# Widening the second score product of differential attention from 64 to 128 contraction rows, in a hybrid decoder layer

## The chip, the cores and the metric

The kernel runs on one core of one Trainium2 chip. The metric is device time in microseconds (us), from the start of the program to its end. The layer has a batch of one, 1024 tokens and a model width of 1024; inputs and outputs are float32.

## The reference: what is computed

One layer normalises the tokens, projects them once with `w_in`, and sends the columns of the projection to three groups of four heads each: mLSTM (a chunkwise matrix memory), differential attention, and cross-attention over 256 memory tokens. Each group is gated by a SiLU of its own columns. The three results are concatenated, mapped back by `w_out`, added to the input and normalised again. The part that the change touches is differential attention:

```python
# q, k: (B, H, 2, S, 64); v: (B, H, S, 128)
for j in range(S_ // Q_BLOCK):                     # 8 blocks of 128 queries
    lo, hi = j * Q_BLOCK, (j + 1) * Q_BLOCK
    s = einsum('bhmqd,bhmkd->bhmqk', q[:, :, :, lo:hi], k[:, :, :, :hi]) * scale
    p = softmax(where(mask, s, -inf), axis=-1)
    pd = p[:, :, 0] - lam * p[:, :, 1]
    outs.append(einsum('bhqk,bhkd->bhqd', pd, v[:, :, :hi]))
```

A head has two maps (m = 0 and 1) with 64 query and key dimensions each. Their softmaxes are subtracted with a learned weight, and the difference is applied to values of width 128. Block j looks at the keys up to its own end, (j+1)·128 of them.

## The kernel before

**Precision by parts.** Most float32 products are made from two rounded parts of each operand. A part "hi" is the value rounded to the multiplier's float32r format, a part "lo" is what the rounding left out. A projection (`proj_T`, L144, and `proj_N`, L153) is 8 contraction blocks times three products (hi·hi, hi·lo, lo·hi): 24 matrix products into one accumulator.

**Order of the work.** The program is written as a list of helper calls, and the framework's planner orders the instructions of every engine by a timeline simulation of its own. On each engine the resulting order is fixed: TensorE (PE) carries out its list strictly in order. So the written order is a priority, and the projections of a later step are used to fill TensorE between the attention blocks of an earlier one. All loads and stores go out from one in-order queue, SyncE's (SP). A tile comes from a pool with a number of buffers per tag (`BUFS`, L27); an instruction that first writes a tile waits until the buffer's last user is done, a DMA included.

**Stages.** First come norms, transposes and the memory cross-attention (L310 to L374), then the value projections `vd_cols` (L473), then differential attention head by head (L493 to L502), then the mLSTM projections (`xm_proj`, `kv_block`, `qk_head`, `gates`, `om_cols`, `zm_half`, L504 to L668), and last, for each of 8 token blocks, the mLSTM chunk, the output projection and the final norm (L679 to the end).

**Differential attention.** `diff_proj(h)` (L380) makes the operands of a head. The query tile `QA[h][m]` has 128 partitions: 64 hold the hi part of map m's queries and the other 64 their lo part. The key tile `KA[h][m]` holds the hi part of the keys in both halves. So one product over 128 partitions gives q_hi·k_hi + q_lo·k_hi (L416). The lo part of the keys, `KB[h]`, is one tile for both maps, map 0 in partitions 0 to 63 and map 1 in 64 to 127; a second product over those 64 partitions adds q_hi·k_lo (L417). A third, in bfloat16, adds the causal mask to the last 128 columns (L419). The key accumulator `kd` is read out by four copies on ScalarE (L397) and, before the change, two subtractions on VectorE (L398) for each half of the tokens.

`diff_block(h, j)` (L400) then takes, for each map, the row maximum (VectorE, L420), its negative scaled (L421), the exponential with row sums (ScalarE, L423), scales and subtracts the two maps (L425 to L429; GpSimd takes L427), transposes the result on TensorE (L436), copies it to SBUF (L438, L440) and multiplies it with the values (L443). The blocks of a head go in the order 0, 7, 1, 6, 2, 5, 3, 4. A score tile of 1024 columns is computed in pieces of up to 512 columns. The score tile has two PSUM buffers, the projections' accumulator `pj` two, all other products two.

**Buffers that the change moves.** Tag `qk` (1032 columns a buffer, 11 of them) holds `QA`, `KA` and `KB`, and before and after that stage the cross-attention's operands, the mLSTM's `xm`, `xcv`, `xh`, `xl`, and in the last stage the chunk's loads (`kvc`, `t1`, `rbc`), `soz` and `xr`. Tag `g` (512 columns, 7 buffers) holds the gates: `szd` (L452, from the gate's projection until `diff_finish` has stored the gated head, L469), `so` (L489), `szm` (L664), and `skc` (L745, loaded for each token block and freed by L763).

Of the kernel before, what the change touches and what calls it, by code (L numbers as in the profile page):

```python
# [8 lines left out]
F32 = mybir.dt.float32  # L9
F32R = mybir.dt.float32r  # L10
BF16 = mybir.dt.bfloat16
AF = mybir.ActivationFunctionType
ALU = mybir.AluOpType
# [10 lines left out]
CS = float(P) ** -0.5  # L24
POOL_LO = ("wkm0", "wkm1")

BUFS = {"h": 16, "w": 8, "g": 7, "qk": 11, "vd": 4, "p": 4, "pT": 2, "od": 2}  # L27
WIDE = ("qk", "od")
C_XM, C_OM, C_ZM, C_QD, C_KD, C_VD, C_ZD, C_QC, C_ZC = [512 * i for i in range(9)]

# [2 lines left out]
def hybrid_layer(ctx: ExitStack, tc: tile.TileContext, x, mem, norm_g, w_in, conv_w, conv_b, wq_m, wk_m,  # L33
# [3 lines left out]
    act, dve, pool, pe = nc.scalar, nc.vector, nc.gpsimd, nc.tensor  # L37
    load = nc.sync.dma_start
    store = nc.sync.dma_start
    x, mem, w_in, w_mem_kv, w_out, out = x[0], mem[0], w_in[0], w_mem_kv[0], w_out[0], out[0]  # L40
# [8 lines left out]
    def slot(tag, name, dt=F32, n=1024):  # L49
        tile_ = big.tile([P, max(n, 1032) if tag in WIDE else n], dt, tag=tag, bufs=BUFS[tag], name=name)  # L50
        return tile_[:, :n] if tag in WIDE else tile_
# [7 lines left out]
    def po(name):  # L59
        return ps.tile([P, 512], F32, tag="o", name=name)  # L60

    def pbig(name):
        return ps.tile([P, 1024], F32, tag="s", name=name)
# [66 lines left out]
    def load_w(tag):  # L130
        i = [e[0] for e in stream].index(tag)
        fetch_w(i + 1 + (tag != "wzc1"))
        kk, wtag = stream[i][2:4]
        hi, lo = [slot(wtag, f"{tag}{part}", F32R) for part in range(2)]
        split_w(hi, lo, raws[tag], pool if tag in POOL_LO else None)
        return [v.rearrange("p (k c) -> p k c", k=kk) for v in (hi, lo)]
# [7 lines left out]
    def proj_T(w, t, tag):  # L144
        acc = pj(tag)
        n = 0
        for k in range(8):
            for wp, hp in ((0, 0), (0, 1), (1, 0)):
                pe.matmul(acc, lhsT=w[wp][:, k, :], rhs=hT_ap(t, k, hp, 0, 512), start=n == 0, stop=n == 23)  # L149
                n += 1  # L150
        return acc
# [14 lines left out]
        store(out=Y[4 * t:4 * t + 4, :, kt, :].rearrange("b p s -> p b s"),  # L166
              in_=ap.rearrange("p (b s) -> p b s", b=4))

# [1 line left out]

    def norm_transpose(src, blocks, g_, tag, sink):
        gbc, gsrc = g_
# [200 lines left out]
        for t in range(2):  # L373
            cross_core(h, t)  # L374

# [1 line left out]
    lo64, hi64 = slice(0, 64), slice(64, 128)  # L377
    QA, KA, KB, od_, ssq_, zg = {}, {}, {}, {}, {}, {}

    def diff_proj(h):  # L380
        w = load_w(f"wqd{h}")
        q = QA[h] = [slot("qk", f"QA{h}{m}", F32R) for m in range(2)]
        for t in range(2):
            c = slice(t * 512, t * 512 + 512)
            acc = proj_T(w, t, f"qd{h}{t}")
            for m, src, oth in ((0, lo64, hi64), (1, hi64, lo64)):
                act.activation(q[m][src, c], acc[src], AF.Copy)
                dve.tensor_tensor(out=q[m][oth, c], in0=acc[src], in1=q[m][src, c].bitcast(F32), op=ALU.subtract)
        w = load_w(f"wkd{h}")
        ka = KA[h] = [slot("qk", f"KA{h}{m}", F32R) for m in range(2)]  # L390
        kb = KB[h] = slot("qk", f"KB{h}", F32R)
        for t in range(2):
            c = slice(t * 512, t * 512 + 512)
            acc = proj_T(w, t, f"kd{h}{t}")
            for m, src, oth in ((0, lo64, hi64), (1, hi64, lo64)):
                for dst in (src, oth):
                    act.activation(ka[m][dst, c], acc[src], AF.Copy)  # L397
                dve.tensor_tensor(out=kb[src, c], in0=acc[src], in1=ka[m][src, c].bitcast(F32), op=ALU.subtract)  # L398

    def diff_block(h, j):  # L400
        if h not in od_:
            od_[h] = slot("od", f"od{h}", n=1032)[:, :1024].rearrange("p (b c) -> p b c", b=NB)
            ssq_[h] = sm.tile([P, NB], F32, tag="dssq", name=f"dssq{h}")
        od, ssq = od_[h], ssq_[h]
        n = (j + 1) * P
        nb = sm.tile([P, 2], F32, tag="dnb", name=f"dnb{h}{j}")
        sums = sm.tile([P, 2], F32, tag="dsum", name=f"dsum{h}{j}")
        pp = []
        for m in range(2):
            sc = pbig(f"ds{h}{j}{m}")  # L410
            lhs = QA[h][m][:, j * P:(j + 1) * P]
            hi = (lo64, hi64)[m]
            for c0 in range(0, n, 512):
                w_ = min(512, n - c0)
                last = c0 + w_ == n
                pe.matmul(sc[:, c0:c0 + w_], lhsT=lhs, rhs=KA[h][m][:, c0:c0 + w_], start=True, stop=False)  # L416
                pe.matmul(sc[:, c0:c0 + w_], lhsT=lhs[hi], rhs=KB[h][hi, c0:c0 + w_], start=False, stop=not last)  # L417
                if last:
                    pe.matmul(sc[:, n - P:n], lhsT=identb, rhs=maskb, start=False, stop=True)  # L419
            dve.tensor_reduce(out=nb[:, m:m + 1], in_=sc[:, :n], op=ALU.max, axis=AX.X)  # L420
            dve.tensor_scalar(out=nb[:, m:m + 1], in0=nb[:, m:m + 1], scalar1=-0.125, scalar2=None, op0=ALU.mult)  # L421
            p_ = slot("p", f"dp{h}{j}{m}")
            act.activation(p_[:, :n], sc[:, :n], AF.Exp, scale=0.125, bias=nb[:, m:m + 1], accum_out=sums[:, m:m + 1])  # L423
            pp.append(p_)
        dve.reciprocal(out=sums, in_=sums)  # L425
        dve.tensor_tensor(out=sums[:, 1:2], in0=sums[:, 1:2], in1=nlam, op=ALU.mult)  # L426
        pool.tensor_scalar(out=pp[1][:, :n], in0=pp[1][:, :n], scalar1=sums[:, 1:2], scalar2=0.0, op0=ALU.mult,  # L427
                           op1=ALU.add)
        dve.scalar_tensor_tensor(out=pp[0][:, :n], in0=pp[0][:, :n], scalar=sums[:, 0:1], in1=pp[1][:, :n],  # L429
                                 op0=ALU.mult, op1=ALU.add)  # L430
        pT = slot("pT", f"dpT{h}{j}")
        for g in range(0, j + 1, 4):
            cnt = min(4, j + 1 - g)
            pt = po(f"dpt{h}{j}{g}")
            for i in range(cnt):
                pe.transpose(out=pt[:, i * P:(i + 1) * P], in_=pp[0][:, (g + i) * P:(g + i + 1) * P], identity=ident)  # L436
            if g:
                dve.tensor_copy(out=pT[:, g * P:(g + cnt) * P], in_=pt[:, :cnt * P])  # L438
            else:
                act.activation(pT[:, g * P:(g + cnt) * P], pt[:, :cnt * P], AF.Copy)  # L440
        acc = po(f"dov{h}{j}")[:, :P]
        for i in range(j + 1):
            pe.matmul(acc, lhsT=pT[:, i * P:(i + 1) * P], rhs=vd[h][:, i, :], start=i == 0, stop=i == j)  # L443
        dve.tensor_copy(out=od[:, j, :], in_=acc)
        sq = sm.tile([P, P], F32, tag="dsq", name=f"dsq{h}{j}", bufs=2)
        act.activation(sq, acc, AF.Square, accum_out=ssq[:, j:j + 1])
# [24 lines left out]
    vd = [slot("vd", f"vd{h}").rearrange("p (b c) -> p b c", b=NB) for h in range(H)]  # L471
# [8 lines left out]
    vd_cols(0, wvd0)  # L480
    vd_cols(1)
    diff_proj(0)
    SOd = [dr.tile([P, 512], F32, name=f"SOd{b}") for b in range(NB)]

    def om_cols(cg):
        w2 = load_w256(f"wom{cg}")
        for b in range(NB):
            acc = proj_N(w2, b, f"om{cg}{b}")
            so = half(f"so{cg}{b}")[:, :256]  # L489
            sigmoid(so, acc, so)  # L490
            store(out=SOd[b][:, cg * 256:(cg + 1) * 256], in_=so)

    for h in range(H):  # L493
        for i, j in enumerate((0, 7, 1, 6, 2, 5, 3, 4)):
            diff_block(h, j)
            if h and i == 2:
                diff_finish(h - 1)
        if h + 1 < H:
            diff_proj(h + 1)
        diff_z(h)  # L500
        if h == 2:
            om_cols(0)  # L502
# [1 line left out]
    xm, xcv = [], []  # L504
    for h in range(H):
        xm.append(slot("qk" if h < 3 else "vd", f"xm{h}"))
# [160 lines left out]
            store(out=SZd[t][:, :, h * P:(h + 1) * P].rearrange("b p s -> p b s"),  # L667
                  in_=sg.rearrange("p (b s) -> p b s", b=4))  # L668

# [1 line left out]
    fg = slot("p", "fg")  # L671
    load(out=fg, in_=final_g.partition_broadcast(P))
    hs = lambda a, h, o=0, n=P, st=P: a[:, o + h * st:o + h * st + n]
# [219 lines left out]
```

## Time and profile before

| | |
|---|---|
| median of 3 runs | 839.0 us (838.33 to 842.41) |
| span of the profiled execution, first to last instruction | 835.7 us |
| median less that span | 3.3 us |
| TensorE matrix products / weight loads, busy | 800.3 us / 662.9 us |
| VectorE / ScalarE / GpSimd, busy | 440.2 us / 323.8 us / 192.8 us |
| mean granted TensorE clock | 0.993 |

The profiled execution's time is known by its span alone; 3.3 us is what the median run has more. Busy shares of TensorE have to be read with care: a matrix product's record runs from its start to a modelled end, so records of neighbours overlap, and what a product really takes of TensorE is the distance from its start to the start of the next. In the listings below "PE" is a matrix product, "PEld" a weight load, DVE VectorE, ACT ScalarE, POOL GpSimd, SPq the queue of DMA issues; an idle time behind a row in brackets names what ended it, and "issue" means that the profile shows nothing that the engine waited for.

### The profile page before, as it was taken

To read this page: it belongs to the slowest core of one execution; us is meant where nothing else is said; L and a number is where in the kernel's file an instruction comes from. 1 tells how busy PE (TensorE), PEld (TensorE's weight loads), DVE (VectorE), ACT (ScalarE), POOL (GpSimd) and SP (SyncE) were. 2 spreads that over 40 slices of the span, in tenths; PEclk is the share of its full clock that TensorE was granted. 3 is DMA by queue.
4 is the path that set the end of the run, shared out by engine and by line. 5 is a ranking of instruction groups with operands and counts; after the bars stand their busy time and mean duration, and the time that the engine had idled before them with its cause. 6 is when DMAs were issued, how large, how long until landed. Compare 5 with 4: busy or idle time off the path is not lost.

```text
span 835.7 us, 11762 instructions
## 1 busy us (share of the span) xinstructions
PE 800.3 (96%) x4432; PEld 662.9 (79%) x4432; DVE 440.2 (53%) x906; ACT 323.8 (39%) x753; POOL 192.8 (23%) x248
## 2 busy tenths in 40 slices
PE   4899999999999999999999999999999789999996
PEld 3788888899977777777789777899878668878886
DVE  5785235343235555655653566654562588666532
ACT  3335234331134444434545434554565333122211
POOL 5433123121111111311312411241323252221000
PEclk9999999999999999999999999999999999999999
DMA  9920212112110000011021111024788999664001
GB/s 254 305 81 18 84 51 76 48 50 68 51 51 26 26 25 27 26 51 38 25 83 56 40 43 59 26 88 159 230 267 292 285 304 302 215 174 156 25 26 51
DMA packets 106416, 89.09 MB, mean 107 GB/s; under 512 B 10480, under 2 KB 91376, under 8 KB 106360
## 3 DMA queue, kind: packets, MB, share of 16 engines
q1 hardware_dynamic: 106216, 88.08, 34.3%
q8 instruction: 35, 0.57, 0.3%
q10 hardware_dynamic: 144, 0.26, 0.1%
q14 instruction: 21, 0.17, 0.1%
HBM read 65.23 MB, written 23.10 MB: 106 GB/s over the span
## 4 chain that ended last, share of the span: by engine, by line
PE 86%; DMA 7%; DVE 2%; SPq 2%; issue 1%; ACT 1%; POOL 1%; POOLq 0%; DVEq 0%; ACTq 0%
PE op L805 13%; PE om L158 5%; PE qd L149 5%; PE kd L149 5%; PE zd L149 5%; PE xm L149 5%; PE vd L158 5%; PE qc L149 5%; PE zc L149 5%; PE zm L149 4%; PE ds L417 4%; PE dov L443 4%; DMA rbc<-RBd 4%; PE ds L416 3%; PE dpt L436 2%
## 5 line engine op out<-in xcount | busy, mean ns | idle before, releaser
L805 PE MATMUL op<-wo,yh 128*128 128x512 f32 (+1 forms) x272 | 83.6, 390 | 1.1 <-DVE szm L666 1.1
L423 ACT ACTIVATE dp<-ds,dnb 128x128 f32<-128x128 f32 (+7 forms) x64 | 47.2, 740 | 68.6 <-DVE dnb L421 62.4
L420 DVE TENSOR_REDUCE dnb<-ds 128x1 f32<-128x128 f32 (+7 forms) x64 | 48.1, 755 | 46.3 <-PE ds L419 46.0
L427 POOL TENSOR_SCALAR dp<-dp,dsum 128x128 f32<-128x128 f32 (+7 forms) x32 | 24.9, 777 | 171.4 <-DVE dsum L426 136.1
L805 PEld LDWEIGHTS op<-wo,yh 128*128 128x128 f32 x272 | 50.5, 192 | 11.7 <-DVE szm L666 1.5
L158 PE MATMUL om<-wom,hT 128*128 128x256 f32 x384 | 54.4, 290 | 0.0
L805 PE MATMUL op<-wo,yl 128*128 128x512 f32 (+1 forms) x136 | 53.0, 390 | 0.0
L149 PE MATMUL qd<-hT,wqd 128*128 128x512 f32 x192 | 50.0, 404 | 0.0
L149 PE MATMUL zd<-hT,wzd 128*128 128x512 f32 x192 | 49.7, 404 | 0.0
L149 PE MATMUL xm<-hT,wxm 128*128 128x512 f32 x192 | 49.6, 404 | 0.0
L149 PE MATMUL zm<-hT,wzm 128*128 128x512 f32 x192 | 47.6, 397 | 2.0 <-POOL wzm L87 2.0
L149 PE MATMUL kd<-hT,wkd 128*128 128x512 f32 x192 | 49.4, 402 | 0.0
L805 PE MATMUL op<-wo,ymr 128*128 128x512 f32 (+1 forms) x204 | 48.3, 384 | 0.0
L158 PEld LDWEIGHTS om<-wom,hT 128*128 128x128 f32 x384 | 48.1, 189 | 0.0
L149 PE MATMUL qc<-hT,wqc 128*128 128x512 f32 x192 | 48.0, 397 | 0.0
L149 PE MATMUL zc<-hT,wzc 128*128 128x512 f32 x192 | 47.5, 397 | 0.0
L158 PE MATMUL vd<-wvd,hT 128*128 128x256 f32 x384 | 47.4, 282 | 0.0
L158 PEld LDWEIGHTS vd<-wvd,hT 128*128 128x128 f32 x384 | 46.3, 188 | 0.3
L149 PEld LDWEIGHTS zm<-hT,wzm 128*128 128x128 f32 x192 | 36.0, 189 | 10.9 <-POOL wzm L87 2.5
L805 PEld LDWEIGHTS op<-wo,ymr 128*128 128x128 f32 x204 | 36.8, 188 | 8.0
L417 PE MATMUL ds<-KB,QA 64*128 64x512 f32 (+3 forms) x96 | 42.2, 439 | 0.0
L149 PEld LDWEIGHTS zc<-hT,wzc 128*128 128x128 f32 x192 | 35.5, 188 | 8.0
(331 smaller groups left out, 1659.9 us busy)
## 6 DMA issues: line engine op xcount, KB each, us to landing
wor<-in_w_out_dram SPq DMA_DIRECT2D x12, 512.0 KB, 5.6
xx<-in_x_dram SPq DMA_DIRECT2D x8, 512.0 KB, 5.9
KVd<-kv SPq DMA_DIRECT2D x8, 512.0 KB, 2.7
QKd<-qkt SPq DMA_DIRECT2D x16, 256.0 KB, 5.1
kvc<-KVd SPq DMA_DIRECT2D x16, 256.0 KB, 7.1
yr<-Yd SPq DMA_DIRECT2D x8, 512.0 KB, 7.7
t<-QKd SPq DMA_DIRECT2D x8, 512.0 KB, 6.3
rbc<-RBd SPq DMA_DIRECT2D x16, 256.0 KB, 9.4
```

Of the source, the lines that this page charges most:

```text
L149: pe.matmul(acc, lhsT=w[wp][:, k, :], rhs=hT_ap(t, k, hp, 0, 512), start=n == 0, stop=n == 23)
L158: pe.matmul(acc, lhsT=hT_ap(b // 4, k, hp, (b % 4) * P, P), rhs=w2[k // 4][wp][:, k % 4, :], start=n == 0, stop=n == 23)
L416: pe.matmul(sc[:, c0:c0 + w_], lhsT=lhs, rhs=KA[h][m][:, c0:c0 + w_], start=True, stop=False)
L417: pe.matmul(sc[:, c0:c0 + w_], lhsT=lhs[hi], rhs=KB[h][hi, c0:c0 + w_], start=False, stop=not last)
L420: dve.tensor_reduce(out=nb[:, m:m + 1], in_=sc[:, :n], op=ALU.max, axis=AX.X)
L423: act.activation(p_[:, :n], sc[:, :n], AF.Exp, scale=0.125, bias=nb[:, m:m + 1], accum_out=sums[:, m:m + 1])
L427: pool.tensor_scalar(out=pp[1][:, :n], in0=pp[1][:, :n], scalar1=sums[:, 1:2], scalar2=0.0, op0=ALU.mult, op1=ALU.add)
L436: pe.transpose(out=pt[:, i * P:(i + 1) * P], in_=pp[0][:, (g + i) * P:(g + i + 1) * P], identity=ident)
L443: pe.matmul(acc, lhsT=pT[:, i * P:(i + 1) * P], rhs=vd[h][:, i, :], start=i == 0, stop=i == j)
L805: pe.matmul(accs[nh][:, c0:c0 + n_], lhsT=yp[a_], rhs=wo[kp, nh, b_][:, o:o + n_], start=k == 2 * KORD[0] and n == 0, stop=k == 2 * KORD[- ...
```

## The change

`KB` becomes one tile for each map, and each holds the lo part of the keys in both halves of its partitions. The second score product then contracts over all 128 partitions with the whole query tile, and gives q_hi·k_lo + q_lo·k_lo. The subtraction that makes `KB` is issued four times for each accumulator, not two. A head holds six `qk` buffers for its operands, not five. To make room, tag `g` has 5 buffers in place of 7, and `qk` 12 in place of 11.

```diff
-BUFS = {"h": 16, "w": 8, "g": 7, "qk": 11, "vd": 4, "p": 4, "pT": 2, "od": 2}
+BUFS = {"h": 16, "w": 8, "g": 5, "qk": 12, "vd": 4, "p": 4, "pT": 2, "od": 2}
...
-        kb = KB[h] = slot("qk", f"KB{h}", F32R)
+        kb = KB[h] = [slot("qk", f"KB{h}{m}", F32R) for m in range(2)]
         for t in range(2):
...
             for m, src, oth in ((0, lo64, hi64), (1, hi64, lo64)):
                 for dst in (src, oth):
                     act.activation(ka[m][dst, c], acc[src], AF.Copy)
-                dve.tensor_tensor(out=kb[src, c], in0=acc[src], in1=ka[m][src, c].bitcast(F32), op=ALU.subtract)
+                for dst in (src, oth):
+                    dve.tensor_tensor(out=kb[m][dst, c], in0=acc[src], in1=ka[m][src, c].bitcast(F32),
+                                      op=ALU.subtract)
...
             lhs = QA[h][m][:, j * P:(j + 1) * P]
-            hi = (lo64, hi64)[m]
...
-                pe.matmul(sc[:, c0:c0 + w_], lhsT=lhs[hi], rhs=KB[h][hi, c0:c0 + w_], start=False, stop=not last)
+                pe.matmul(sc[:, c0:c0 + w_], lhsT=lhs, rhs=KB[h][m][:, c0:c0 + w_], start=False, stop=not last)
```

## The prediction

> **What bounds the kernel now.** I read the engines' shares first, then the chain of work that ended last, then the busy times by stretch, cut at the first and the last score product.
>
> ```profile
> span 835.7 us, 11762 instructions
> ...
> PE 800.3 (96%) x4432; PEld 662.9 (79%) x4432; DVE 440.2 (53%) x906; ACT 323.8 (39%) x753; POOL 192.8 (23%) x248
> ...
> PE 86%; DMA 7%; DVE 2%; SPq 2%; issue 1%; ACT 1%; POOL 1%; POOLq 0%; DVEq 0%; ACTq 0%
> ```
>
> ```profile
> 243.90:521.10 277.20, 277.20 (x1447) 211.52 (x1445) 154.07 (x324) 124.65 (x306) 58.05 (x75) 1.00 0.14 41
> 0.00:243.90 243.90, 227.78 (x1380) 200.90 (x1381) 109.76 (x178) 81.28 (x205) 61.40 (x78) 1.00 0.32 95
> 521.10:600.00 78.90, 78.90 (x525) 71.78 (x525) 40.60 (x70) 42.34 (x85) 23.16 (x24) 1.00 0.33 114
> 600.00:760.00 160.00, 147.03 (x729) 120.19 (x727) 105.05 (x255) 62.03 (x123) 44.09 (x62) 0.97 0.83 254
> ```
>
> The columns of the second view are the stretch, its length, busy times of PE, PEld, DVE, ACT and POOL, the granted clock, the DMA engines' share and GB/s. In the 277.2 us from 243.9 to 521.1, where all score products lie, PE is never without a product in flight, at full clock, while DVE is busy 154.07 us of it (56%), ACT 124.65 and the DMA engines 14%. TensorE alone sets the time there, so what a product costs it is paid in full. The stretch from 600 to 760 is another matter: DMA engines 83% busy, PE idle for 160 − 147.0 = 13 us.
>
> A full PE need not be an efficient one. The waits of the weight loads in the attention stretch show it; "issue" means that nothing in the profile accounts for the wait:
>
> ```profile
> PEld ds L417 <- issue: 20.0, 74, 0.4
> ...
> PEld ds L416 <- issue: 7.1, 29, 0.2
> ...
> PEld L419 <- issue: 6.7, 31, 0.3
> ```
>
> The weight loader stands still for 20.0 us ahead of the 64-row load of L417 (74 times), and for 7.1 and 6.7 us ahead of the loads of L416 and L419, 33.8 us in all. The timelines of the loads and of the products around 270 us show where:
>
> ```profile
> 270.58 0.18 PEld L417 LDWEIGHTS ds<-KB,QA 64*128 64x128 f32 x1 [0.36 <-issue]
> 271.00 0.19 PEld L416 LDWEIGHTS ds<-KA,QA 128*128 128x128 f32 x1 [0.24 <-issue]
> ```
>
> ```profile
> 270.26 0.39 PE L416 MATMUL ds<-KA,QA 128*128 128x512 f32 x1
> 270.58 0.50 PE L417 MATMUL ds<-KB,QA 64*128 64x512 f32 x1
> 271.01 0.45 PE L416 MATMUL ds<-KA,QA 128*128 128x384 f32 x1
> 271.38 0.44 PE L417 MATMUL ds<-KB,QA 64*128 64x384 f32 x1
> 271.75 0.23 PE L419 MATMUL ds<-maskb,identb 128*128 128x128 bf16 x1
> 271.79 0.48 PE L416 MATMUL ds<-KA,QA 128*128 128x512 f32 x1
> ```
>
> The load of the 64-row weights begins only at 270.58, 0.32 us after the 128-row product began, and the next 128-row load only at 271.00, 0.42 us after the 64-row one began. Going from 128 rows to 64, and back, is not overlapped. Products of 128 rows follow each other faster; three rows of the chain give their pace:
>
> ```profile
> 64.84 5.60 PE qc L149 x24
> ...
> 193.68 28.16 PE vd L158 x240
> ...
> 397.42 0.89 PE dov L443 x8
> ```
>
> That is 233 ns for 512 columns, 117 ns for 256 and 111 ns for 128. For 384 no row stands; 175 ns is the middle of 117 and 233.
>
> **The change part by part.** *The second product.* After the change L417 has the form that L416 has. Whether it then streams at the pace above, although it has L416's own weights and adds into the same accumulator, can be read where the mLSTM's product does the same: `xh` and `xl` take the same weights, one after the other.
>
> ```profile
> 597.54 0.39 PE L550 MATMUL qk<-xh,wqk 128*128 128x512 f32 x1
> 597.77 0.40 PE L550 MATMUL qk<-xl,wqk 128*128 128x512 f32 x1
> 598.01 0.39 PE L550 MATMUL qk<-xh,wqk 128*128 128x512 f32 x1
> ```
>
> 0.23 and 0.24 us from start to start: full pace. So I cost each piece, now and after, by starts. A piece of 512 with more behind it (270.26 to 271.01) takes 0.75 us and will take 2 × 0.233 = 0.466: −0.28. A second piece of 384 (271.01 to 271.75) takes 0.74, will take 0.35: −0.39. Narrow blocks, from the first score product to the mask product:
>
> ```profile
> 262.49 0.28 PE L416 MATMUL ds<-KA,QA 128*128 128x256 f32 x1
> ...
> 263.01 0.23 PE L419 MATMUL ds<-maskb,identb 128*128 128x128 bf16 x1
> ...
> 280.87 0.34 PE L416 MATMUL ds<-KA,QA 128*128 128x384 f32 x1
> ...
> 281.50 0.23 PE L419 MATMUL ds<-maskb,identb 128*128 128x128 bf16 x1
> ...
> 313.21 0.30 PE L416 MATMUL ds<-KA,QA 128*128 128x128 f32 x1
> ...
> 313.70 0.23 PE L419 MATMUL ds<-maskb,identb 128*128 128x128 bf16 x1
> ```
>
> 256 columns take 0.52 us, will take 0.234: −0.29. 384 take 0.63, will take 0.35: −0.28. 128 take 0.49, will take 0.22: −0.27. For one map of one head the eight blocks then save 0.27 (j=0) + 0.29 + 0.28 + 0.28 (j=3, one piece of 512) + 0.55 (j=4, 512 and 128) + 3 × 0.67 (j=5 to 7, where I take the 0.28 + 0.39 of j=6 for all three) = 3.68 us. Times 2 maps and 4 heads: **29.4 us**. The loader's 33.8 us of standing still is a bound from above; the 20.0 us ahead of L417 alone, if the other two stalls should stay, is the bound from below.
>
> *The mask product* (L419) stays. Its price behind a 128-row product shows once, where the planner put it behind L443:
>
> ```profile
> 282.72 0.71 PE L443 MATMUL dov<-vd,dpT 128*128 128x128 f32 x4
> 283.27 0.22 PE L419 MATMUL ds<-maskb,identb 128*128 128x128 bf16 x1
> 283.30 0.48 PE L149 MATMUL zd<-hT,wzd 128*128 128x512 f32 x1
> ```
>
> The next product starts 0.03 us after it, against 0.04 us at 271.75, so I count no difference.
>
> A page of the Trainium skill speaks against this step: "TensorE: Matmul & The Clock Gate", Part 3 (packing small matmuls), says that a weight load overlaps a product in flight only where the two use different row groups. By it a load for all 128 rows could never hide behind a 128-row product, and the change would save nothing here. The trace does not agree: the products of L149 start 0.233 us apart (5.60 us for 24), less than one load and one stream end to end would need.
>
> *The added subtractions.* 16 more of this row:
>
> ```profile
> L398 DVE TENSOR_TENSOR KB<-kd,KA 64x512 fp32r<-64x512 f32 x16 | 11.0, 687 | 8.3 <-ACT KA L397 8.1
> ```
>
> 16 × 0.687 = 11.0 us on DVE. DVE goes from 154.07 to 165 us in a stretch of 277 − 29 = 248 us, 67%: the load is covered by PE's other work. What can show is latency. ACT and DVE take turns on the accumulator, so `kd` is given back 2 × 0.687 = 1.4 us later, and the head's first scores may be 1.4 us later, each for 8 accumulators. The tightest place that I found is head 3, whose last subtraction and whose buffer's next user (the second `zd` product) are:
>
> ```profile
> 402.71 0.69 DVE L398 TENSOR_TENSOR KB<-kd,KA 64x512 fp32r<-64x512 f32 x1
> ...
> 405.94 0.94 PE L149 MATMUL zd<-hT,wzd 128*128 128x512 f32 x3
> ```
>
> 405.94 − 403.40 = 2.5 us of slack, less 1.4, less some 0.6 that two narrower scores between them save: 0.5 us is left. If the cover were gone everywhere it would cost 8 × 1.4 = 11 us; with slack left even there the sum is nearer to nothing, and I take 1.5 us.
>
> *The buffers.* During attention two heads need 12 `qk` buffers, as they needed 10 of 11: still two heads, no spare. In `g`, two heads' `szd` hold four, which leaves one for `so` while the output gates of `om_cols(0)` fill PE, not three: a microsecond or two on ACT, covered by 2.8 us or more of PE for each accumulator (24 × 0.117). In the last stage a 12th `qk` buffer lets a chunk's load go out sooner, and two `g` buffers fewer make `szm` and `skc` wait for each other. Neither has a row that prices it; the bound to both sides is one late load of the chain:
>
> ```profile
> 644.36 11.39 DMA rbc<-RBd
> 658.15 10.48 DMA rbc<-RBd
> ```
>
> From −10.5 to +11.4 us, taken as 0, since the two pull in opposite ways. All of the planner's order is made anew, too, which no row can price; I hold it to be inside these bounds.
>
> The sum is 835.7 − 29.4 + 1.5 = 807.8 us of span, and with the 3.3 us by which the median run (839.0) exceeds the profiled span **811 us**.
>
> **The rivals.** *Given back to VectorE.* DVE carries out its list in order, and a `KB` subtraction that the planner places ahead of a due row maximum (L420) delays that block's exponential by 0.69 us. If all 16 land so and PE, now faster, waits each time, the whole 11.0 us shows: 839.0 − 29.4 + 1.5 + 11.0 = 822 us. For it speaks the two-buffer score tile; against it DVE at 67%, and that PE now waits for nothing in the stretch.
>
> *The relief does not come.* If the load of L417 waits because it comes second on weights in use, and not because of its 64 rows, nothing is saved: 839.0 + 1.5 = 840 us. For it speaks only that every L417 follows L416 or fillers of the same array; the L550 rows speak against it. (This is what the rule of the Trainium skill named above would make of it.)
>
> *A better last stage.* If the 12th buffer takes the shorter of the two `rbc` waits off the chain: 811 − 10.5 = 801 us.
>
> *Slower: the gate buffers block SP's queue.* Before, seven `g` buffers take `szm` and the loads of `skc` up to block 7 without waiting:
>
> ```profile
> L746 SPq DMA_DIRECT2D skc<-SKd x8: 319/424/2034, 620.9 to 678.9; - x8
> ```
>
> All eight are issued by 678.9 us. With five, `skc5` to `skc7` wait until an earlier block has used its own, and if the planner puts them ahead of a chunk's loads in the in-order queue, `kvc`, `t` and `rbc` behind them are late by as much. From the point at which three chunks each lose one 11.39 us load, it costs 34 us: 811 + 34 = 845 us. Against it: the planner knows the buffers and can issue later, when DMA is less loaded.
>
> **How the numbers follow.** The forecast, 811 us (own range 802 to 820: the 20.0 and 33.8 us bounds of the saving give 820.5 and 806.7, and half of the last stage's bound goes below), has a chance of 0.63; VectorE's 822 0.17; the better last stage 0.07; no relief 0.06; slower 0.07. The range 798 to 828 takes in the first three with some room and leaves out 0.13 and the far ends of the others. What a measurement of this kernel can tell from no change is about 0.5%, 4.2 us: faster by more 0.87, within it 0.06 (no relief), slower 0.07.
>
> **What would show it.** Right, if in the profile after the L417 products read 128*128 and start 0.23 us after L416 at 512 columns, if the weight loader's idle "issue" time at L416, L417 and L419 is nearly gone, if first to last score product takes some 248 us with PE still without waits, and if the stage behind keeps its length. Wrong, if L417 keeps 0.4 us from start to start (no relief); if PE shows waits for DVE `dnb`, `KB` or ACT `dp` (VectorE); if after the mLSTM projections PE's idle time grows by tens of us with SP waiting at L746 (gate buffers).

## The result

The changed kernel takes 819.4 us (819.14 to 819.9) against 840.7 us for the kernel before: a ratio of 0.9755, interval 0.9731 to 0.9779. Forecast were 811 us, in a range of 798 to 828. The direction, the cause and the range held; the gain is 21 us (0.0245 × 840.7 = 20.6), not 28, so some 7 us of the forecast gain are to be found.

### The profile after

The page of the changed kernel, span, engines and chain:

```profile
span 817.7 us, 11784 instructions
...
PE 770.1 (94%) x4432; PEld 663.9 (81%) x4432; DVE 445.2 (54%) x922; ACT 322.3 (39%) x753; POOL 192.6 (24%) x248
...
PE 76%; DMA 11%; DVE 4%; issue 3%; POOL 2%; SPq 2%; ACT 2%; POOLq 0%; DVEq 0%; ACTq 0%
```

TensorE's share of the chain has fallen from 86% to 76% and the transfers' has risen from 7% to 11%. The lines of the score products are now L417 (first), L418 (second) and L420 (mask). The timeline of PE at the block with two pieces of 512 columns, and at the narrowest block:

```profile
239.81 0.22 PE L417 MATMUL ds<-KA,QA 128*128 128x128 f32 x1
239.87 0.28 PE L418 MATMUL ds<-KB,QA 128*128 128x128 f32 x1
239.98 0.23 PE L420 MATMUL ds<-maskb,identb 128*128 128x128 bf16 x1
...
245.69 0.39 PE L417 MATMUL ds<-KA,QA 128*128 128x512 f32 x1
245.92 0.39 PE L418 MATMUL ds<-KB,QA 128*128 128x512 f32 x1
246.15 0.62 PE L417 MATMUL ds<-KA,QA 128*128 128x512 f32 x2
```

The second product now follows the first after 0.23 us, as every 128-row product does, where the 64-row one came 0.32 us after it and held the next back by 0.43 us. The narrow block takes 0.17 us up to its mask, in place of 0.49. The weight loader's waits in the attention stretch of the changed kernel say the same:

```profile
PEld L420 <- issue: 6.1, 28, 0.3
PEld ds L417 <- ACT dp L424: 1.7, 1, 1.7
```

The 20.0 us ahead of the second product and the 7.1 us ahead of the first are gone. The 6.7 us ahead of the mask's load stay, as 6.1 us: this stall does not belong to the 64 rows.

To see where the time went I divided both profiles at the same four events: the first and last score product, and the first and last product of the `zm` gates. The last two stretches, before and after (columns: stretch, length, busy PE, PEld, DVE, ACT, POOL, clock, DMA share, GB/s):

```profile
583.60:648.30 64.70, 62.64 (x286) 50.17 (x284) 31.73 (x40) 38.43 (x64) 19.71 (x18) 0.97 0.82 259
648.30:835.70 187.40, 170.14 (x876) 141.97 (x876) 111.38 (x308) 45.79 (x113) 38.33 (x59) 0.98 0.55 170
```

```profile
548.70:634.50 85.80, 71.35 (x331) 57.09 (x330) 37.90 (x57) 40.52 (x71) 20.67 (x24) 0.92 0.80 239
634.50:817.70 183.20, 165.82 (x852) 138.24 (x851) 104.56 (x296) 44.65 (x110) 36.73 (x53) 0.98 0.52 159
```

| stretch, by PE's products | before, us | after, us | difference | PE idle, before and after |
|---|---|---|---|---|
| start to first score product | 244.1 | 239.8 | −4.3 | 16.1, 13.6 |
| first to last score product | 277.3 | 254.2 | −23.1 | 0, 2.2 |
| to the first `zm` product | 62.2 | 54.7 | −7.5 | 0, 0 |
| first to last `zm` product | 64.7 | 85.8 | +21.1 | 2.1, 14.4 |
| to the end | 187.4 | 183.2 | −4.2 | 17.3, 17.4 |
| span | 835.7 | 817.7 | −18.0 | 35.4, 47.6 |

The stretches do not hold the same work, because the planner ordered everything anew: some 20 more products lie between the first and the last score product than before, and 45 more in the `zm` stretch (331 against 286). So lengths alone mislead, and PE's idle time is the safer reading: the span falls by 18.0 us because PE is busy 30.2 us less (770.1 against 800.3) and idle 12.2 us more.

Three things were not forecast. Time is won where the change touches nothing, before the first score product (−4.3 us). In the attention stretch, forecast at some 248 us without waits, PE now waits 2.2 us, and with the 20 products more it takes 254.2 us. And the `zm` stretch is 21.1 us longer: 8.7 us of that is work moved into it, and 12.4 us is PE standing idle (85.8 − 71.35 = 14.4 us; before, 2.1 us). Its mean clock is 0.92 in place of 0.97. PE's waits in the changed kernel and VectorE's timeline show what holds the gates up:

```profile
PE zm L149 <- DVE szm L667: 8.1, 2, 5.7
```

```profile
619.56 0.87 DVE L699 TENSOR_SCALAR rbc<-rbc,colA 128x128 f32<-128x128 f32 x4 [7.59 <-DMA rbc<-RBd]
622.96 0.69 DVE L705 TENSOR_TENSOR rbc<-t,rbc 128x512 f32<-128x512 f32 x1 [2.52 <-DMA rbc<-RBd]
623.57 0.68 DVE L667 TENSOR_TENSOR szm<-zm,szm 128x512 f32<-128x512 f32 x1
```

The multiplication L667 frees the accumulator that PE's next `zm` product needs. In VectorE's list it stands behind a chunk's work on `rbc`, which waits 7.59 and 2.52 us for transfers. ScalarE had its operand ready long before, at 614.2 us:

```profile
613.55 0.63 ACT L93 ACTIVATE szm<-szm 128x512 f32<-128x512 f32 x1
```

PE's own timeline has the other end of it, 5.72 us of standing still:

```profile
624.30 5.66 PE L149 MATMUL zm<-hT,wzm 128*128 128x512 f32 x16 [5.72 <-DVE szm L667]
```

### The profile page after: what moved, and what is told of

It reads as the page before. It is cut to its first block, busy times and chain, and to the rows that moved or that the text cites. A ratio compares the mean times of both kernels' runs of the same rounds, so it can differ in the third digit from the quotient of the medians.

```text
span 817.7 us, 11784 instructions
## 1 busy us (share of the span) xinstructions
PE 770.1 (94%) x4432; PEld 663.9 (81%) x4432; DVE 445.2 (54%) x922; ACT 322.3 (39%) x753; POOL 192.6 (24%) x248
## 4 chain that ended last, share of the span: by engine, by line
PE 76%; DMA 11%; DVE 4%; issue 3%; POOL 2%; SPq 2%; ACT 2%; POOLq 0%; DVEq 0%; ACTq 0%
PE op L806 8%; PE om L158 6%; PE zd L149 5%; PE kd L149 5%; PE xm L149 5%; PE qd L149 5%; DMA rbc<-RBd 5%; PE qc L149 5%; PE zc L149 5%; PE vd L158 5%; PE zm L149 4%; PE dov L444 4%; PE ds L417 2%; PE ds L418 2%; PE dpt L437 2%
## 5 line engine op out<-in xcount | busy, mean ns | idle before, releaser
L149 PE MATMUL zm<-hT,wzm 128*128 128x512 f32 x192 | 51.0, 421 | 11.0 <-DVE szm L667 8.1
L806 PEld LDWEIGHTS op<-wo,yh 128*128 128x128 f32 x272 | 50.6, 193 | 12.5 <-DVE szm L667 2.8
L428 POOL TENSOR_SCALAR dp<-dp,dsum 128x128 f32<-128x128 f32 (+7 forms) x32 | 27.0, 844 | 135.8 <-DVE dsum L427 90.6
L149 PEld LDWEIGHTS zm<-hT,wzm 128*128 128x128 f32 x192 | 38.6, 205 | 20.4 <-DVE szm L667 8.7
L158 PE MATMUL om<-wom,hT 128*128 128x256 f32 x384 | 52.4, 287 | 0.0
L149 PE MATMUL qd<-hT,wqd 128*128 128x512 f32 x192 | 48.3, 399 | 0.0
L149 PEld LDWEIGHTS qc<-hT,wqc 128*128 128x128 f32 x192 | 35.5, 188 | 7.3
```

Of the source, the lines that this page charges most:

```text
L158: pe.matmul(acc, lhsT=hT_ap(b // 4, k, hp, (b % 4) * P, P), rhs=w2[k // 4][wp][:, k % 4, :], start=n == 0, stop=n == 23)
L806: pe.matmul(accs[nh][:, c0:c0 + n_], lhsT=yp[a_], rhs=wo[kp, nh, b_][:, o:o + n_], start=k == 2 * KORD[0] and n == 0, stop=k == 2 * KORD[- ...
```

## The experiments

Each run is compared with the kernel before on the same chip; the ratio is to that.

**1. The rows alone.** The shared `KB` tile, old buffers, no added subtraction; only the second product is widened. Its extra term is a product of two rounding remainders.

```diff
-                pe.matmul(sc[:, c0:c0 + w_], lhsT=lhs[hi], rhs=KB[h][hi, c0:c0 + w_], start=False, stop=not last)
+                pe.matmul(sc[:, c0:c0 + w_], lhsT=lhs, rhs=KB[h][:, c0:c0 + w_], start=False, stop=not last)
```

> Before, with one edit: the second score product contracts over all 128 partitions of the query tile and of the one shared KB tile, so it adds q_hi*k_lo + q_lo*(the other map's k_lo); the last term is a product of two rounding remainders. No added subtraction, no added buffer, old buffer counts. Both theories: the score products lose the same 28.6 us of start-to-start time as in the changed kernel. Theory A (the new buffer counts give time back in the last stage): nothing is given back, 840.7 - 29 = about 811 us. Theory B (the last stage gives back whatever it is handed, because its transfers and their order bound it): about 820 us, as the changed kernel. Theory C (the 16 added subtractions give it back): about 811 us.

Measured: 806.0 us against 835.6, ratio 0.9648 (0.9607 to 0.9690), 29.6 us faster. The prediction's 29.4 us for the rows is met, and the last stage gives nothing back:

```profile
244.20:491.40 247.20, 247.20 (x1448) 209.90 (x1447) 152.24 (x323) 123.82 (x304) 58.41 (x75) 1.00 0.15 45
553.60:616.90 63.30, 61.28 (x286) 48.84 (x284) 31.49 (x39) 37.57 (x63) 20.30 (x18) 1.00 0.82 258
616.90:803.10 186.20, 169.82 (x877) 142.07 (x876) 111.90 (x308) 46.75 (x115) 39.16 (x59) 0.98 0.55 174
```

The attention stretch falls by 30.1 us and the `zm` stretch keeps its length (63.3 us). Theory B, a last stage that absorbs whatever it is given, falls.

**2. The buffers alone.** Before, with the new counts.

```diff
-BUFS = {"h": 16, "w": 8, "g": 7, "qk": 11, "vd": 4, "p": 4, "pT": 2, "od": 2}
+BUFS = {"h": 16, "w": 8, "g": 5, "qk": 12, "vd": 4, "p": 4, "pT": 2, "od": 2}
```

> Before, with the new buffer counts alone (g 5, qk 12). Theory A: slower than before by what the last stage lost in the changed kernel, 840.7 + 10 to 17 = 851 to 858 us, with the products of zm waiting for szm. Theories B and C: the same as before, 838 to 843 us.

Measured: 847.1 us against 835.6, ratio 1.0128 (1.0092 to 1.0164): 11.4 us slower. The `zm` stretch is the changed kernel's:

```profile
576.60:663.50 86.90, 71.35 (x331) 57.37 (x330) 37.38 (x57) 41.34 (x75) 21.09 (x24) 0.92 0.77 239
```

Theory A holds, at the low end. The stretch is 22 us longer, but again it holds 45 products more than before (331 against 286); PE is idle 15.5 us in it, against 2.1, and there PE waits 8.4 us for `szm`, as in the changed kernel. The first stages got faster again, which experiments 5 to 7 take up.

**3. The change with the old buffers** (g 7, qk 11).

> The changed kernel with the old buffer counts (g 7, qk 11). Theory A: the last stage is as long as before, 811 to 813 us. Theories B and C: about 820 us. If the sixth operand buffer of a head matters (11 buffers do not hold two heads' twelve), PE waits for QA or KB between heads and it is above 820 us.

Measured: 825.8 us, ratio 0.9888 (0.9849 to 0.9926), slower than with the new counts. The `zm` stretch is as before (64.7 us), but the attention stretch is longer, as the last sentence of the expectation has it:

```profile
242.60:508.00 265.40, 251.86 (x1441) 212.12 (x1440) 159.54 (x336) 122.77 (x303) 55.98 (x75) 0.99 0.14 41
```

PE is idle 13.5 us in it. The waits are not the expected ones: PE waits almost wholly for the softmax's work on VectorE and ScalarE (4.4 us of it for L422), and only 0.4 us at `KB`. Experiment 1, with five operand tiles a head and the same eleven buffers, has no idle time there, and the added subtractions cost nothing (experiment 9). So the cause, that two heads' twelve operand tiles do not fit into eleven buffers, is found by exclusion and not seen as a wait. With `KB` as two tiles the 12th buffer pays, and what it costs elsewhere is part of the price.

**4. The rows alone, with the new buffers.** Experiment 1 with the counts of experiment 2.

> The first of these kernels (128 rows on the shared KB tile) with the new buffer counts (g 5, qk 12). Theory A: about 820 us, the changed kernel's time. Theory B: about 820 us. Theory C: about 811 us, since there are no added subtractions.

Measured: 814.1 us, ratio 0.9729 (0.9688 to 0.9769); the `zm` stretch takes 87.5 us. Against experiment 1 the buffers cost 0.8% here, 7 to 8 us. The changed kernel's ratio, 0.9755, is 0.3% above, inside the intervals, so what is left for the subtractions and the sixth operand tile together is small.

**5, 6, 7. Where the tiles start.** The 12th `qk` buffer is 4128 bytes long. All tags laid out behind it (`p`, `pT`, `w`, `g`) move by 4128, so their start moves by 32 bytes modulo 64. The token tiles `hT` stay. In all kernels so far the pace of the products went with that (512 columns every 232 ns with the old place, every 229 with the new), so I moved the tiles by unused 32-byte tiles and nothing else, on the kernel of experiment 1. For 5:

```diff
+    padb = big.tile([P, 8], F32, tag="padb", bufs=1, name="padb")
+    pool.memset(padb, 0.0)
     norm_transpose(mem, range(2), (mgbc, mem_norm_g), "m", m_sink)
```

For 6 the same two lines, as `pada`, stand ahead of `mT`, the first of the large tiles; for 7 both.

> The 128-row product on the shared KB tile (old buffer counts, ratio 0.965 to before) with an unused 32-byte tile put in front of the tags p, pT, w and g, which moves the weight tiles from a multiple of 64 bytes to 32 beyond one, as the 12th qk buffer of 4128 bytes does in the change. The token tiles hT lie 32 beyond a multiple of 64 in both. Theory L (the start of the tiles sets the pace): products of 512 columns go every 229 ns in place of 232, of 256 columns every 113 to 114 in place of 117, and the time falls by about 8 us, ratio 0.955. Theory N (the pace that differed came with the planner's order): 232 ns and ratio 0.965.

> The same with the 32-byte tile in front of all large tiles: hT now starts on a multiple of 64 bytes and the weights 32 beyond one. Theory L1 (weights and tokens must have the same phase): slow pace, 232 ns, ratio 0.965. Theory L2 (the weights' own phase decides): 229 ns, ratio 0.955. Theory N: 232 ns, ratio 0.965.

> Both 32-byte tiles: hT and the weights start on a multiple of 64 bytes. Theory L1 (same phase): 229 ns, ratio 0.955. Theory L2 (weights 32 beyond): 232 ns, ratio 0.965. Theory N: 232 ns, ratio 0.965.

| kernel | `hT` modulo 64 | weights modulo 64 | 24 × 10 `vd` products, us | ratio (interval) |
|---|---|---|---|---|
| experiment 1 | 32 | 0 | not on its chain (117 ns from start to start) | 0.9648 (0.9607 to 0.9690) |
| 5 | 32 | 32 | 27.22 | 0.957 (0.954 to 0.960) |
| 6 | 0 | 32 | 28.16 | 0.966 (0.9638 to 0.9682) |
| 7 | 0 | 0 | 27.23 | 0.9542 (0.9522 to 0.9562) |

The same row of the chain in 5, 6 and 7, one fence each; the kernel before has 28.16 and the changed one 27.21:

```profile
190.55 27.22 PE vd L158 x240
```

```profile
192.86 28.16 PE vd L158 x240
```

```profile
191.86 27.23 PE vd L158 x240
```

Theory L1 holds and L2 and N fall: what counts is that the two operands of a product have the same start modulo 64 bytes. Products of 512 columns then start every 229 ns, not 232 (medians of the starts before the attention), and of 256 columns every 113 to 114 ns, not 117. The order of the instructions on PE, VectorE, ScalarE and SP is in 5, 6 and 7, one by one, that of experiment 1, so the planner's order is not what changed the pace. The time won before the first score product comes with it: that stretch takes 239.6 us in experiment 5 and 244.2 in experiment 1. Experiment 7 takes 799.0 us against 836.8; it beats both kernels.

**8. The gate buffers alone.** Experiment 1 with 5 buffers in `g` and `qk` left at 11; the weights stay in place.

> The 128-row product on the shared KB tile with the gate tag cut from 7 to 5 buffers and qk left at 11; the weights stay where they were. Theory A1 (the gate buffers cost the last stage its time): the last stage, from the first zm product to the end, is 15 to 20 us longer than with 7, ratio 0.965 + 0.02 = 0.985. Theory A2 (the 12th qk buffer costs it, because the planner then puts chunk loads and their VectorE work ahead of the gates): the last stage keeps its length, ratio 0.965.

Measured: 814.7 us, ratio 0.973 (0.9702 to 0.9759), 0.8% above experiment 1.

```profile
551.40:626.20 74.80, 67.78 (x306) 52.76 (x304) 33.48 (x44) 39.67 (x68) 16.96 (x18) 0.95 0.74 233
```

The `zm` stretch is 11.5 us longer than in experiment 1, but it also holds 20 products more (306 against 286). By PE's idle time from the first `zm` product to the end, experiment 1 has 18.4 us, this run 25.0 and experiment 4 30.7. So neither theory has it alone: the two gate buffers cost 6.6 us, and the 12th `qk` buffer, added to that, 5.7 us. The two do not act by the same wait. PE's wait for `szm`, here and in experiment 4:

```profile
PE zm L149 <- DVE szm L665: 0.3, 1, 0.3
```

```profile
PE zm L149 <- DVE szm L665: 8.0, 2, 5.5
```

The wait for VectorE's multiplication comes only with the 12th buffer. What the gate buffers cost is spread over several waits (3.0 us of it the `qk` products' for ScalarE's copies, in the `zm` stretch), and no run takes them apart. The ratio of experiment 4, 0.9729, is no worse than this run's, although PE idles longer there: the 12th buffer also moves the tiles to the better start.

**9. The subtractions alone.** Experiment 1, with each subtraction issued twice into the same place.

```diff
-                dve.tensor_tensor(out=kb[src, c], in0=acc[src], in1=ka[m][src, c].bitcast(F32), op=ALU.subtract)
+                for _ in range(2):
+                    dve.tensor_tensor(out=kb[src, c], in0=acc[src], in1=ka[m][src, c].bitcast(F32), op=ALU.subtract)
```

> The 128-row product on the shared KB tile with old buffers, and each subtraction that makes KB issued twice into the same place: the 16 added VectorE instructions of the change and nothing else of it. The prediction's step: 1.5 us, ratio 0.965 + 0.002 = 0.967. The rival that all 11.0 us show: ratio 0.978, with PE waits for VectorE in the attention stretch. No cost at all: 0.965.

Measured: 805.3 us, ratio 0.960 (0.9568 to 0.9631). The groups' row has the added instructions, and the attention stretch does not feel them:

```profile
L399 DVE TENSOR_TENSOR KB<-kd,KA 64x512 fp32r<-64x512 f32 x32 | 21.9, 686 | 8.0 <-ACT KA L397 7.5
```

```profile
243.40:490.70 247.30, 247.30 (x1448) 209.97 (x1447) 162.46 (x337) 123.07 (x304) 56.46 (x75) 1.00 0.15 45
```

247.3 us against 247.2 without them, PE never idle, with 10 us more of VectorE's time. They cost nothing that can be measured; the rival "given back to VectorE" falls.

**10. The gates first in the written order.** Experiment 4, with `zm_half(0)` ahead of the first two chunks.

```diff
+    zm_half(0)
     chunk(0)
     chunk(1)
-    zm_half(0)
     chunk_out(0)
```

> The 128-row product on the shared KB tile with the new buffer counts (ratio 0.973), and in the written order the first half of the zm gates moved ahead of the first two chunks. Theory P (the 12th qk buffer lets the planner put the first chunk's loads and their VectorE work ahead of the gates, and the gates' accumulators wait behind it): the stretch of the zm products falls from 87 us towards 64 to 75, ratio 0.955 to 0.964. Theory D (the transfers of the last stage bound it, whatever the order): ratio 0.973, the first chunk only moves later.

Measured: 815.6 us, ratio 0.9732 (0.9696 to 0.9768); the `zm` stretch takes 87.1 us. That settles nothing between P and D: the order of the instructions came out the same as in experiment 4, one by one, on all five engines, so this run is experiment 4 once more, and the written order was not the lever that I took it for. Why the planner puts the chunk's work ahead of the gates when there is a 12th buffer stays open.

**11, 12. The place of the tiles, in the two kernels themselves.** The changed kernel with the 32-byte tile of experiment 5, which takes the same start away from it, and the kernel before with both 32-byte tiles, which gives it.

> The changed kernel with an unused 32-byte tile in front of the tags p, pT, w and g, which takes the weights back to a multiple of 64 bytes while hT stays 32 beyond one. Theory L1 (weights and tokens must have the same phase): the 512-column products go back to 232 ns and the change loses some 8 us, ratio 0.9755 + 0.009 = 0.985. Theory N (no effect of the start): 0.9755.

> The kernel before with both 32-byte tiles and nothing else, so that weights and hT start on a multiple of 64 bytes. Theory L1: 229 ns for 512 columns, about 8 us faster, ratio 0.989 to 0.991. Theory N: ratio 1.000.

Measured: the changed kernel becomes slower, ratio 0.9812 (0.9782 to 0.9842) against 0.9755; the kernel before becomes faster, 830.0 us against 837.5, ratio 0.9921 (0.9882 to 0.9960). The `vd` row is 28.40 us in the first and 27.23 us in the second. L1 holds in both; the loss in the changed kernel is 0.6%, not the 0.9% expected, because the stretch from the first `zm` product to the end is 4.4 us shorter there (264.6 against 269.0); what shortens it is not shown. The order of the instructions on PE, VectorE, ScalarE and SP is again that of the kernel without the 32-byte tiles, in both.

## Why the prediction was right, and where not

**The rows.** Right, in cause and size. The second product reads 128*128 and follows after 0.23 us, as was named as a sign. From start to next start, first and second score products took 65.6 us before and 37.0 us after (summed over all 96 of each in the trace): 28.6 us for the 29.4 forecast; alone they bring 29.6 us (experiment 1). The bound from below, in which only the 20.0 us ahead of L417 go, was not needed: the stall ahead of L416 went too, and only the mask's stayed. The rule weighed there, from the Trainium skill's "TensorE: Matmul & The Clock Gate", Part 3, that a load hides behind a product only for other row groups, does not hold here: L418's products follow L417's on the same 128 rows after 0.23 us.

**The subtractions.** Forecast 1.5 us, measured none (experiment 9): PE never waits in that run's attention stretch, so the cover that the prediction saw was enough there. In the changed kernel itself PE waits 2.2 us in the stretch. The rival in which VectorE takes 11.0 us back named waits for `dnb`, `KB` or `dp` as its sign: of these there is one, 1.5 us for ScalarE's `dp`.

**The operand buffers.** Forecast "still two heads, no spare", at no cost. Between experiment 4 and the change, which differ by the sixth tile of a head and the subtractions, the first `zm` product comes 3.2 us later (548.7 against 545.5) and the ratio rises by 0.0026. That is inside the intervals; since the subtractions alone cost nothing, the sixth tile is what is left for it, by exclusion only. The 2.2 us that PE waits in the changed kernel's attention stretch are not in experiment 4 and fall under the same head.

**The last stage** is the step that failed. It was taken as 0, "since the two pull in opposite ways". They did not: from the first `zm` product to the end, fewer `g` buffers make PE idle 6.6 us more (experiment 8), and the 12th `qk` buffer 5.7 us more on top, where it was to bring a gain. In the changed kernel that part takes 16.9 us more (269.0 against 252.1), of which 12.5 us is idle time of PE and the rest work that lay ahead of it before. The rival that named this place had the wrong mechanism, SP's queue held up at the loads of `skc`: up to the last `zm` product no such load waits for a buffer, and behind it one waits 3.1 us. What waits with the 12th buffer is PE, on an accumulator, because VectorE's work for the gates stands in its list behind work that waits for transfers. And the rival's price, 34 us, was more than twice what came.

**What was not in the sum** is the place of the tiles. The same 12th buffer moved the weights to the start that `hT` has modulo 64 bytes, and this gave back part: 5 to 9 us by the ratios of experiments 5, 7, 11 and 12. Net, the buffers cost 11.4 us on the kernel before (experiment 2) and 7 to 8 us on the rows alone (experiment 4). With 29.6 us for the rows this leaves 18 to 23 us; 21 were measured.

That the time still lies inside the narrower range, 802 to 820 us, is in part luck. Its upper end was worked out from a smaller saving at the score products, which did not come; what took the time was the last stage, and a gain that was not forecast, the place of the tiles, made up for some of it.

## What to carry to other kernels

A product on part of the rows in a stream of full ones was here not cheaper but dearer: read its cost from start to start, and widen it if the operand can be made to hold something harmless in the other rows. Here the shared tile did that without the second copy of `KB`, so the buffers could have stayed, and the simpler kernel is 1.1% faster than the one that was made (ratios to the kernel before of 0.9648 and 0.9755). A buffer count is never a free part of an edit: it changes what a later stage can prefetch, the planner's order, and where every tile behind it lies. And when a planner orders the work anew, compare the idle time of the engine that sets the time, not the lengths of stretches that no longer hold the same work.

## What was not expected of the hardware

The pace of a matrix product depends on where its two operands start. With the tiles of the stationary and the moving operand at the same place modulo 64 bytes, 512 float32r columns go every 229 ns and 256 every 113 to 114 ns; 32 bytes apart it is 232 ns (234 in experiment 11) and 117 ns. Two unused 32-byte tiles make the kernel before 0.8% faster (ratio 0.9921, 0.9882 to 0.9960). Only shifts of 32 bytes were tried, so whether other distances matter is open, as is the cause. And the weight loader stalls ahead of the bfloat16 mask product, whether that follows a product of 64 rows or of 128: 6.7 us before and 6.1 us after, over 64 products. Whether the change of data type is the cause, no run shows.
